# Block-diagonal gate products of a recurrence: one head on 128 rows of the array, or two heads on 64 rows each

## The chip, the cores and the metric

The kernel runs on one core of a Trainium2 chip. The metric is the device time of one execution in microseconds; the median of three runs stands for a kernel. One more execution was recorded by the hardware profiler. Busy time, waits and the order of events below come from that recording. Its engines are TensorE (PE, with its weight loads shown apart as PEld), VectorE (DVE), ScalarE (ACT), GpSimd (POOL) and SyncE (SP), which issues most of the DMAs.

## The reference

One layer of a hybrid backbone is computed for 128 prompt tokens and 512 latent tokens together (640 columns), width 1024. After a norm and the input projection one branch is a bidirectional gated linear recurrence (RG-LRU); beside it run a gated linear attention (GLA) and, behind both, an output projection and an MLP. What is touched here are the recurrence's two gates, a block-diagonal product with 16 blocks (heads) of 64 by 64 per direction:

```
def blockdiag(x, w):
    xb = x.reshape(*x.shape[:-1], LRU_BLOCKS, LRU_BW)      # 16 heads of 64
    return jnp.einsum('...nc,ncd->...nd', xb, w).reshape(x.shape)

r = sigmoid(blockdiag(xc, wa) + ba);  i = sigmoid(blockdiag(xc, wx) + bx)
a = exp(-8 * r * softplus(-L));       u = sqrt(1 - a * a) * (i * xc)
h[t] = a[t] * h[t-1] + u[t]           # forwards and backwards; the two are added
```

All arithmetic of the reference is float32.

## The kernel before

**Matrix products in parts.** A float32 operand is split in two parts of the faster type float32r: a high part (a cast on ACT) and the rest (a subtraction on DVE). A dense product is three matmuls, high by high, high by low, low by high. The dense work of this stretch is the input projection: `dense<-HH,whi`, `dense<-HL,whi`, `dense<-HH,wlo` on 128 rows, 128 columns and 320 tokens each, in PSUM tiles of their own pool (`psd`, two tiles).

**The recurrence.** Features lie on partitions. A group `f` of 128 features holds two heads `b` of 64; there are eight groups and two directions `d`, so 16 pairs (f, d), called directions below. `lru_chain` makes for each group a `prep` stage, two `gates` stages and then decay, inputs, drive and scans. `prep(f)` loads the weights of both heads and directions, gate r and gate i side by side, into `bdr` (the load for the next group is issued by `bd_load`, from POOL after the first group). For each head the 64 features of `xc[f]` are laid on 128 partitions: the high part on the head's own half (`A.copy`), the low part on the other half (`V.tensor_tensor`); this tile is `xs`. The head's weights stand on both halves of `bdr`, split into `bh` and `bl`. So a matmul with `bh` gives the high weights by (high + low) input and one with `bl` the low weights by the same: four products in two matmuls over the full 128 rows, for one head. `gates(f, d)` does this for both heads, each in one tile of the PSUM pool `psa`, which has two tiles named `aux` and serves the GLA stages and transposes too. Each head's result is 64 rows of r over 64 rows of i; a sigmoid on ACT takes it out of PSUM, and three DMAs on SP put the halves together, so that `r` and `i` hold 128 features each.

**The order of the work.** All operations are recorded first, then a planner (`Recorder.order`) goes through them with an estimated cost for each (`Recorder.cost`) and a model of free tiles, and so writes the order of each engine's queue. PE, ACT, DVE and SP then run their queues strictly in that order. All instructions of the profile therefore carry the line of one helper, L343 (L342 for some table loads). The planner lets a matmul of the gates go as soon as an `aux` tile is thought free, between the dense matmuls.

The steps that the change touches are the tile `bdr` and `bd_load` (from line 673), `prep` (line 1102) and `gates` (line 1116) in `lru_chain`, and the planner's cost of a float32r matmul (line 138).

Of the kernel before, what the change touches and what calls it, by code (L numbers as in the profile page):

```python
# [8 lines left out]
F32 = mybir.dt.float32  # L9
F32R = mybir.dt.float32r  # L10
I32 = mybir.dt.int32
AF = mybir.ActivationFunctionType
OP = mybir.AluOpType
# [5 lines left out]
T = 640  # L19
# [90 lines left out]
class Recorder:  # L110
# [21 lines left out]
    @staticmethod  # L132
    def cost(eng, name, args, kw, out):
        n = _dims(out)
        if eng == "PE":
            if name == "transpose":
                return max(0.05, n * 2 / 2400)
            if args[1].dtype == F32R:
                return max(n / 2400 + 0.0025, 0.106)
            if out.ap[0][1] <= 32 and n >= 128:  # L140
                return n / 2400 + 0.0025
            return max(0.213, n * 4 / 2400)
        aps = [a for a in list(args[1:]) + list(kw.values()) if hasattr(a, "ap")]
        scalars = sum(_dims(a) == 1 for a in aps) if n > 1 else 0
        sbuf = all(a.space == bass.MemoryType.SB for a in aps)
        if eng == "ACT":
            if name == "dma_start":
                return 0.1
            return (0.093 if sbuf else 0.051) + n / 1200 + 0.094 * scalars
        if eng == "DVE":  # L150
            if name == "reciprocal":
                return 6.25e-3 * n
            fast = name in ("tensor_copy", "tensor_scalar", "memset") and sbuf and out.space == bass.MemoryType.SB
            return 0.068 + n / (1920 if fast else 960) + 0.061 * scalars
        if eng == "POOL":
            if name == "dma_start":
                return 1.0
            if name in ("memset", "affine_select"):
                return 0.03 + n * 0.0009
            if name == "tensor_copy":  # L160
                return 0.1 + n * 0.0034
            return 0.1 + n * (0.008 if name == "tensor_scalar" and n < 64 else 0.0022) + (0.35 if kw.get("op") == OP.pow else 0.06)
        return 0.63 if kw["in_"].space == bass.MemoryType.SB else 0.5
# [228 lines left out]
def tile_hybrid_layer(  # L392
# [8 lines left out]
    V, A, PE, G, SP = (Port(rec, e) for e in ("DVE", "ACT", "PE", "POOL", "SP"))  # L401

    consts = ctx.enter_context(tc.tile_pool(name="consts", bufs=1))
# [11 lines left out]
    def t_(name, dt=F32):  # L415
        return rec.tile(tp, N_T, [128, TW], dt, name, "t")
# [7 lines left out]
    def aux():  # L424
        return rec.tile(psa, 2, [128, 2, 512], F32, "aux", "a")
# [10 lines left out]
    f32 = lambda ap: ap.bitcast(F32)  # L436
# [83 lines left out]
    ps = aux()  # L520
# [21 lines left out]
    ps = aux()  # L542
# [61 lines left out]
    def split_act(src, hi, lo):  # L604
        A.copy(hi, src)
        V.tensor_tensor(lo, src, f32(hi), op=OP.subtract)
# [63 lines left out]
        by[MH_ENG[3]].tensor_tensor(HL[:, k, :], x[:, 0:T], f32(HH[:, k, :]), op=OP.subtract)  # L670


    bdr = consts.tile([128, 2, 2, 128], F32, name="bdr")

    def bd_load(f):
        for g, w in enumerate((lru_wa, lru_wx)):
            for b in range(2):
                for r in range(2):
                    (G if f else SP).dma_start(out=bdr[64 * r:64 * (r + 1), b, :, 64 * g:64 * (g + 1)],
                                             in_=w[0, :, 2 * f + b].rearrange("d c e -> c d e"))  # L680


    n8sp = consts.tile([128, 16], F32, name="n8sp")
# [74 lines left out]
    units, posted = [], set()  # L758
# [25 lines left out]
    xc, ya = [None] * KT, [None] * KT  # L784
# [161 lines left out]
    def parts(src, name):  # L946
        n = src.shape[-1]
        hi, lo = t_(name + "h", F32R), t_(name + "l", F32R)
        split_act(src, hi[:, 0:n], lo[:, 0:n])
        return hi, lo  # L950
# [147 lines left out]
    def lru_chain(j):  # L1098
        s = {}
        fs = (2 * j, 2 * j + 1)  # L1100

        def prep(f):
            def fn():

                bh, bl, xs = t_("bh", F32R), t_("bl", F32R), (t_("xs", F32R), t_("xs", F32R))
                split_act(bdr.rearrange("p b d e -> p (b d e)"), bh[:, 0:512], bl[:, 0:512])
                for b, x in enumerate(xs):
                    hi, lo = slice(64 * b, 64 * (b + 1)), slice(64 * (1 - b), 64 * (2 - b))
                    A.copy(x[hi, 0:T], xc[f][hi, 0:T])
                    V.tensor_tensor(x[lo, 0:T], xc[f][hi, 0:T], f32(x[hi, 0:T]), op=OP.subtract)  # L1110
                s["in", f] = (bh, bl, xs)
                if f + 1 < KT:
                    bd_load(f + 1)
            return Stage(fn, 2.1, 2.0, lambda: f"zx{f}" in posted)

        def gates(f, d):
            def fn():
                bh, bl, xs = s["in", f]
                out = []
                for b in range(2):  # L1120
                    ps, m = aux(), slice(128 * (2 * b + d), 128 * (2 * b + d + 1))
                    for n, w in enumerate((bh, bl)):
                        for i in range(2):
                            PE.matmul(ps[:, i, 0:320], w[:, m], xs[b][:, 320 * i:320 * (i + 1)], start=n == 0, stop=n == 1)
                    g = t_("r")
                    act(h2(g), pv(ps), AF.Sigmoid, bias=bgate(d, 2 * f + b))
                    out.append(g)

                r, i_, th = out[0], t_("i"), t_("th")
                top, end = slice(0, 64), slice(64, 128)  # L1130
                SP.dma_start(out=i_[top, 0:T], in_=r[end, 0:T])
                SP.dma_start(out=i_[end, 0:T], in_=out[1][end, 0:T])
                SP.dma_start(out=r[end, 0:T], in_=out[1][top, 0:T])
                act(th[:, 0:T], r[:, 0:T], AF.Tanh, scale=p4sp[:, 8 * d + f:8 * d + f + 1])
                V.tensor_tensor(i_[:, 0:T], i_[:, 0:T], xc[f][:, 0:T], op=OP.mult)
                s["r", f, d], s["i", f, d], s["th", f, d] = r, i_, th
            return Stage(fn, 0.75, 2.5)

        def decay():
            for f in fs:  # L1140
                for d in range(2):
                    r = s["r", f, d]
                    act(r[:, 0:T], r[:, 0:T], AF.Exp, scale=n8sp[:, 8 * d + f:8 * d + f + 1])

        def inputs():
            for f in fs:
                for d in range(2):
                    th = s["th", f, d]
                    act(th[:, 0:T], th[:, 0:T], AF.Sqrt)

        def drive(f):
            def fn():
                for d in range(2):
                    r, i_, th = s["r", f, d][:, 0:T], s["i", f, d][:, 0:T], s["th", f, d][:, 0:T]
                    V.scalar_tensor_tensor(th, r, 1.0, th, op0=OP.add, op1=OP.mult)
                    V.tensor_tensor(th, th, i_, op=OP.mult)
            return Stage(fn, 3.0, 0.0)

        def scans(f):
            def fn():  # L1160
                for d in range(2):
                    a, u, h = s["r", f, d], s["th", f, d], s["i", f, d]
                    for sl, init in ((slice(0, 128), 0.0), (slice(128, T), h0(d, f))):
                        av, uv, hv = a[:, sl], u[:, sl], h[:, sl]
                        if d:
                            av, uv, hv = av[:, ::-1], uv[:, ::-1], hv[:, ::-1]
                        V.tensor_tensor_scan(hv, av, uv, init, op0=OP.mult, op1=OP.add)
                    e = 127 * (1 - d)
                    V.tensor_copy(nst[:, 8 * d + f:8 * d + f + 1], h[:, e:e + 1])
                ya[f] = s["i", f, 0]  # L1170
                V.tensor_tensor(ya[f][:, 0:T], ya[f][:, 0:T], s["i", f, 1][:, 0:T], op=OP.add)
                if f == KT - 1:
                    ps = aux()
                    PE.transpose(ps[0:16, 0, 0:128], nst, ident)
                    o = t_("nsto")
                    V.tensor_copy(o[0:16, 0:128], ps[0:16, 0, 0:128])
                    SP.dma_start(out=new_lru[0, 0].rearrange("d (k p) -> (d k) p", p=128), in_=o[0:16, 0:128])
            return Stage(fn, 2.5, 0.0)

        prev = lru_list[-1] if lru_list else None  # L1180
        lru_list.append(Chain("lru", [
            prep(fs[0]), gates(fs[0], 0), gates(fs[0], 1), prep(fs[1]), gates(fs[1], 0), gates(fs[1], 1),
            Stage(decay, 0.0, 2.9), Stage(inputs, 0.0, 2.9), drive(fs[0]), drive(fs[1]), scans(fs[0]), scans(fs[1])],
            after=lambda: prev is None or prev.done))
# [658 lines left out]
```

## Time and profile before

| | |
|---|---|
| median of three runs | 1139.33 us (1138.63 to 1140.05) |
| profiled execution | 1140.71 us, span 1138.8 us |
| PE busy | 1109.5 us, 97% of the span, 7020 matmuls |
| ACT busy | 616.1 us (54%) |
| DVE busy | 848.1 us (74%) |
| gates: matmuls | 128, from 72.8 to 239 us |

The span is the time from the first to the last instruction; the profiled execution's own time is 1.9 us more. Matmuls overlap in the array, so the duration of one (about 310 ns for 320 columns) isn't what it costs; the distance between the starts of two that follow each other is. A wait in the profile is idle time of an engine together with what ended it.

### The profile page before, as it was taken

To read this page: it belongs to the slowest core of one execution; us is meant where nothing else is said; L and a number is where in the kernel's file an instruction comes from. 1 tells how busy PE (TensorE), PEld (TensorE's weight loads), DVE (VectorE), ACT (ScalarE), POOL (GpSimd) and SP (SyncE) were. 2 spreads that over 40 slices of the span, in tenths; PEclk is the share of its full clock that TensorE was granted. 3 is DMA by queue.
4 is the path that set the end of the run, shared out by engine and by line. 5 is a ranking of instruction groups with operands and counts; after the bars stand their busy time and mean duration, and the time that the engine had idled before them with its cause. 6 is when DMAs were issued, how large, how long until landed. Compare 5 with 4: busy or idle time off the path is not lost.

```text
span 1138.8 us, 17811 instructions
## 1 busy us (share of the span) xinstructions
PE 1109.5 (97%) x7020; PEld 1042.9 (92%) x7020; DVE 848.1 (74%) x1363; ACT 616.1 (54%) x998; POOL 78.6 (7%) x152
## 2 busy tenths in 40 slices
PE   6999999999999999999999999999999999999996
PEld 5799898999999999999999988888898899899895
DVE  4686875868474837727996559997779989987767
ACT  5387988895475748611433358744444433333442
POOL 3135103000000000000000011000000000000001
PEclk9999999999999999999999999999999999999998
DMA  9835426251221212227544456422233333222422
GB/s 293 265 74 150 122 66 173 56 163 38 94 75 56 75 57 74 75 74 232 195 157 167 130 184 207 145 75 74 74 123 122 110 118 137 95 75 74 154 88 93
DMA packets 104476, 136.94 MB, mean 120 GB/s; under 512 B 8179, under 2 KB 78021, under 8 KB 104393
## 3 DMA queue, kind: packets, MB, share of 16 engines
q1 hardware_dynamic: 102344, 133.91, 37.8%
q0 software_dynamic: 2048, 1.90, 0.7%
q8 instruction: 55, 0.90, 0.3%
q14 instruction: 29, 0.23, 0.1%
HBM read 121.61 MB, written 6.31 MB: 112 GB/s over the span
## 4 chain that ended last, share of the span: by engine, by line
PE 77%; DVE 9%; ACT 6%; DMA 4%; issue 3%; POOL 0%; SPq 0%; DVEq 0%; POOLq 0%; ACTq 0%
PE dense L343 52%; PE aux L343 25%; DVE i L343 3%; DVE th L343 2%; DMA modw<-in_w_mod_dram 1%; DVE wlo L343 1%; ACT r L343 1%; DMA i<-r 1%; ACT L343 1%; ACT th L343 1%; DMA r<-r 1%; DMA raw<-in_w_in_dram 1%; DMA w2raw<-in_gla_w_dram 1%; ACT whi L343 1%; ACT L342 1%
## 5 line engine op out<-in xcount | busy, mean ns | idle before, releaser
L343 ACT CAST whi<-raw 128x1024 fp32r<-128x1024 f32 (+2 forms) x173 | 167.1, 970 | 289.3 <-PE dense L343 141.5
L343 DVE TENSOR_TENSOR wlo<-raw,whi 128x1024 fp32r<-128x1024 f32 (+1 forms) x168 | 190.1, 1133 | 75.8 <-ACT whi L343 75.0
L343 PE MATMUL dense<-HH,whi 128*128 128x320 f32 x768 | 179.0, 313 | 0.5 <-DVE g L343 0.3
L343 PE MATMUL dense<-HL,whi 128*128 128x320 f32 x768 | 176.5, 310 | 0.0
L343 PE MATMUL dense<-HH,wlo 128*128 128x320 f32 x752 | 172.8, 310 | 0.0
L343 PEld LDWEIGHTS dense<-HH,whi 128*128 128x128 f32 x768 | 129.2, 189 | 2.6 <-issue 0.8
L343 PEld LDWEIGHTS dense<-HL,whi 128*128 128x128 f32 x768 | 129.4, 189 | 0.0
L343 PEld LDWEIGHTS dense<-HH,wlo 128*128 128x128 f32 x752 | 126.4, 189 | 0.0
L343 PE MATMUL dense<-whi,ah 128*128 128x512 f32 (+1 forms) x288 | 113.0, 392 | 0.0
L343 PE MATMUL dense<-wlo,ah 128*128 128x512 f32 (+1 forms) x288 | 113.0, 392 | 0.0
L343 PE MATMUL dense<-whi,al 128*128 128x512 f32 (+1 forms) x288 | 113.0, 392 | 0.0
L343 DVE SCALAR_TENSOR_TENSOR mac<-mw,cst,mac 128x512 f32<-128x512 f32 x112 | 78.1, 746 | 0.0
L343 PE MATMUL aux<-H2H,whi 128*128 128x320 f32 (+1 forms) x240 | 74.8, 311 | 0.0
L343 PE MATMUL aux<-H2L,whi 128*128 128x320 f32 (+1 forms) x240 | 74.7, 311 | 0.0
L343 PE MATMUL aux<-H2H,wlo 128*128 128x320 f32 (+1 forms) x240 | 74.6, 311 | 0.0
L343 PEld LDWEIGHTS dense<-whi,al 128*128 128x128 f32 x288 | 54.1, 188 | 12.5
L343 PEld LDWEIGHTS dense<-whi,ah 128*128 128x128 f32 x288 | 54.1, 188 | 10.3
L343 PEld LDWEIGHTS dense<-wlo,ah 128*128 128x128 f32 x288 | 54.1, 188 | 10.2
L343 ACT CAST whi<-s 128x512 fp32r<-128x512 f32 x42 | 26.0, 619 | 67.1 <-PE aux L343 62.9
L343 PE MATMUL aux<-f,whi 128*128 128x320 f32 x224 | 59.4, 308 | 0.0
L343 DVE TENSOR_TENSOR fa<-fa,dense 128x512 f32<-128x512 f32 x66 | 45.2, 686 | 17.8 <-PE dense L343 17.6
L343 PE MATMUL aux<-f,wlo 128*128 128x320 f32 x168 | 51.9, 309 | 0.0
(335 smaller groups left out, 2500.1 us busy)
## 6 DMA issues: line engine op xcount, KB each, us to landing
raw<-in_mlp_w_dram SPq DMA_DIRECT2D x34, 1024.0 KB, 5.0
raw<-in_w_in_dram SPq DMA_DIRECT2D x24, 1024.0 KB, 5.3
mw<-in_w_mod_dram SPq DMA_DIRECT2D x64, 256.0 KB, 5.4
modw<-in_w_mod_dram SPq DMA_DIRECT2D x32, 256.0 KB, 5.9
raw<-in_w_out_dram SPq DMA_DIRECT2D x8, 1024.0 KB, 4.8
i<-r SPq DMA_DIRECT2D x32, 160.0 KB, 2.4
raw<-in_w_in_dram SPq DMA_DIRECT2D x8, 512.0 KB, 4.6
raw<-in_lru_up_dram SPq DMA_DIRECT2D x4, 1024.0 KB, 4.9
```

The source lines that it names most:

```text
L342: nc.scalar.preload_act_table_set("natural_log_exp_and_others")
L343: getattr(eng[o.eng], o.name)(*o.args, **o.kw)
```

## The change

The two heads of a group are no longer multiplied one after the other over 128 rows. Each head gets 64 rows of the array: `xc[f]` is split as it stands, into `xsh` and `xsl` with both heads on their own halves, and so are the weights, now without the second copy (`bdr`, `bh`, `bl` have 256 columns in place of 512, and a group's weights come in four DMAs in place of eight). A direction then takes three products for each head, 12 matmuls of 64 rows in place of 8 of 128 rows, in which the two heads alternate. Both PSUM tiles are taken at the start, and the sigmoids follow behind all 12. The low-by-low product, which before came along, is left out. The planner gets a cost for a float32r matmul of 64 rows: half that of its columns.

```
             if name == "transpose":
                 return max(0.05, n * 2 / 2400)
+            if args[1].dtype == F32R and args[1].ap[0][1] == 64 and n >= 128:
+                return n / 4800 + 0.0025
...
-    bdr = consts.tile([128, 2, 2, 128], F32, name="bdr")
+    bdr = consts.tile([128, 2, 128], F32, name="bdr")
...
-                for r in range(2):
-                    (G if f else SP).dma_start(out=bdr[64 * r:64 * (r + 1), b, :, 64 * g:64 * (g + 1)],
-                                             in_=w[0, :, 2 * f + b].rearrange("d c e -> c d e"))
+                (G if f else SP).dma_start(out=bdr[64 * b:64 * (b + 1), :, 64 * g:64 * (g + 1)],
+                                           in_=w[0, :, 2 * f + b].rearrange("d c e -> c d e"))
...
-                bh, bl, xs = t_("bh", F32R), t_("bl", F32R), (t_("xs", F32R), t_("xs", F32R))
-                split_act(bdr.rearrange("p b d e -> p (b d e)"), bh[:, 0:512], bl[:, 0:512])
-                for b, x in enumerate(xs):
-                    hi, lo = slice(64 * b, 64 * (b + 1)), slice(64 * (1 - b), 64 * (2 - b))
-                    A.copy(x[hi, 0:T], xc[f][hi, 0:T])
-                    V.tensor_tensor(x[lo, 0:T], xc[f][hi, 0:T], f32(x[hi, 0:T]), op=OP.subtract)
-                s["in", f] = (bh, bl, xs)
+                bh, bl = t_("bh", F32R), t_("bl", F32R)
+                split_act(bdr.rearrange("p d e -> p (d e)"), bh[:, 0:256], bl[:, 0:256])
+                s["in", f] = (bh, bl) + parts(xc[f][:, 0:T], "xs")
...
-                for b in range(2):
-                    ps, m = aux(), slice(128 * (2 * b + d), 128 * (2 * b + d + 1))
-                    for n, w in enumerate((bh, bl)):
-                        for i in range(2):
-                            PE.matmul(ps[:, i, 0:320], w[:, m], xs[b][:, 320 * i:320 * (i + 1)], start=n == 0, stop=n == 1)
+                out, pss, m = [], [aux(), aux()], slice(128 * d, 128 * (d + 1))
+
+                for n, (w, x) in enumerate(((bh, xh), (bh, xl), (bl, xh))):
+                    for i in range(2):
+                        for b, ps in enumerate(pss):
+                            r = slice(64 * b, 64 * (b + 1))
+                            PE.matmul(ps[:, i, 0:320], w[r, m], x[r, 320 * i:320 * (i + 1)], start=n == 0, stop=n == 2)
+                for b, ps in enumerate(pss):
                     g = t_("r")
                     act(h2(g), pv(ps), AF.Sigmoid, bias=bgate(d, 2 * f + b))
```

The planner's order changes with it. Two places on PE show the two forms that a direction takes. The first is group 1, forward, among the dense matmuls of the input projection; before:

```order
L343 MATMUL dense<-HL,whi 128x320 x2
L343 MATMUL dense<-HH,wlo 128x320 x2
L343 MATMUL aux<-xs,bh 128x320 x2
L343 MATMUL aux<-xs,bl 128x320 x2
L343 MATMUL aux<-xs,bh 128x320 x2
L343 MATMUL aux<-xs,bl 128x320 x2
L343 MATMUL dense<-HH,whi 128x320 x2
```

and in the changed kernel, whose helper has line 345:

```order
L345 MATMUL dense<-HL,whi 128x320 x2
L345 MATMUL dense<-HH,wlo 128x320 x2
L345 MATMUL aux<-xsh,bh 128x320 x4
L345 MATMUL aux<-xsl,bh 128x320 x4
L345 MATMUL aux<-xsh,bl 128x320 x4
L345 MATMUL dense<-HH,whi 128x320 x2
```

Eight matmuls in a row have become twelve, and the four of a row go to the heads in turn: head 0, head 1, head 0, head 1. 12 of the 16 directions stand in this way; one of them is in two pieces with dense matmuls between, and in another the first four go head 0 twice, head 1 twice.

The second place is group 2, backward, where the numbers tell the two heads' PSUM tiles apart (305 and 307 before, 310 and 311 now); before:

```order
L343 MATMUL aux_305<-xs_290,bh_288 128x320 x2
L343 MATMUL aux_305<-xs_290,bl_289 128x320 x2
L343 MATMUL dense_299<-HH_127,whi_282 128x320
L343 MATMUL aux_307<-xs_291,bh_288 128x320 x2
L343 MATMUL aux_307<-xs_291,bl_289 128x320 x2
L343 MATMUL dense_299<-HH_127,whi_282 128x320
```

and in the changed kernel:

```order
L345 MATMUL aux_310<-xsh_290,bh_288 128x320 x2
L345 MATMUL aux_310<-xsl_291,bh_288 128x320 x2
L345 MATMUL aux_310<-xsh_290,bl_289 128x320 x2
L345 MATMUL dense_304<-HH_127,wlo_283 128x320
L345 MATMUL dense_321<-whi_286,HH_127 128x256
L345 MATMUL dense_321<-wlo_287,HH_127 128x256
L345 MATMUL aux_311<-xsh_290,bh_288 128x320 x2
L345 MATMUL aux_311<-xsl_291,bh_288 128x320 x2
L345 MATMUL aux_311<-xsh_290,bl_289 128x320 x2
```

Here the planner lets head 0 go as soon as its tile is free and head 1 later, with dense matmuls between: six matmuls on one half of the array, then six on the other. Four directions stand in this way (the tiles 233/234, 310/311, 399/400 and 466/467).

The third place is the queue of SP around group 5, whose halves are put together by the DMAs `i<-r` and `r<-r`; `raw` is a load of weights of 1 MB. Before (direction backward, r_368 and r_370 are the two heads):

```order
L343 DMA r_359<-r_361 64x640
L343 DMA i_371<-r_368 64x640
L343 DMA raw_376<-in_w_in_dram 128x8x256
L343 DMA i_371<-r_370 64x640
L343 DMA r_368<-r_370 64x640
L343 DMA raw_401<-in_w_in_dram 128x8x256
```

and in the changed kernel (r_380 and r_381):

```order
L345 DMA r_362<-r_363 64x640
L345 DMA raw_377<-in_w_in_dram 128x8x256
L345 DMA i_382<-r_380 64x640
L345 DMA i_382<-r_381 64x640
L345 DMA r_380<-r_381 64x640
L345 DMA raw_408<-in_w_in_dram 128x8x256
```

The load that stood between the first and the second DMA of the exchange stands ahead of all three.

## Rows read from the trace of the kernel before

**Rows 1.** The page: busy time of each engine, share of the span, instructions.

```profile
PE 1109.5 (97%) x7020; PEld 1042.9 (92%) x7020; DVE 848.1 (74%) x1363; ACT 616.1 (54%) x998; POOL 78.6 (7%) x152
PE 77%; DVE 9%; ACT 6%; DMA 4%; issue 3%; POOL 0%; SPq 0%; DVEq 0%; POOLq 0%; ACTq 0%
```

**Rows 2.** Stretches with gates: busy by engine (instructions), granted clock, DMA share.

```profile
60.00:120.00 60.00, 60.00 (x411) 59.92 (x410) 47.88 (x70) 49.65 (x76) 25.41 (x57) 1.00 0.47 122
120.00:180.00 60.00, 57.02 (x397) 56.11 (x396) 48.32 (x68) 52.09 (x61) 9.30 (x16) 0.97 0.46 113
180.00:245.00 65.00, 61.34 (x429) 60.47 (x428) 48.34 (x71) 59.01 (x72) 4.68 (x8) 0.97 0.44 116
```

**Rows 3.** Waits of PE, 60 to 245 us: total, times, longest.

```profile
PE aux L343 <- ACT r L343: 6.0, 4, 2.7
PE dense L343 <- DVE g L343: 0.3, 1, 0.3
```

**Rows 4.** Instructions on `xs` and `bh`: count, ns least/median/most, first and last start.

```profile
L343 PE MATMUL aux<-xs,bh x64: 302/309/634, 72.8 to 239.0; 128*128 128x320 f32 x64
L343 PE MATMUL aux<-xs,bl x64: 303/309/468, 73.1 to 239.3; 128*128 128x320 f32 x64
L343 ACT CAST xs<-xc x16: 710/725/733, 67.7 to 221.7; 64x640 fp32r<-64x640 f32 x16
L343 DVE TENSOR_TENSOR xs<-xc,xs x16: 818/820/883, 71.1 to 225.0; 64x640 fp32r<-64x640 f32 x16
L343 ACT CAST bh<-bdr x8: 605/613/624, 46.9 to 216.5; 128x512 fp32r<-128x512 f32 x8
L343 DVE TENSOR_TENSOR bl<-bdr,bh x8: 681/688/693, 47.6 to 223.4; 128x512 fp32r<-128x512 f32 x8
```

**Rows 5.** PE in order of time: one direction (start us, us, instruction).

```profile
113.94 0.46 PE L343 MATMUL aux<-xs,bh 128*128 128x320 f32 x2
114.23 0.45 PE L343 MATMUL aux<-xs,bl 128*128 128x320 f32 x2
...
115.11 0.46 PE L343 MATMUL dense<-HH,whi 128*128 128x320 f32 x2
```

**Rows 6.** PE in order of time: matmuls on a quarter of the array's columns (128*32).

```profile
38.12 0.46 PE L343 MATMUL dense<-HH,wlo 128*128 128x320 f32 x2
38.62 1.93 PE L343 MATMUL aux<-modw,cst 128*32 128x256 f32 x32
40.48 0.56 PE L343 MATMUL dense<-HH,whi 128*128 128x320 f32 x2
40.88 0.31 PE L343 MATMUL dense<-HL,whi 128*128 128x320 f32 x1
...
44.85 0.45 PE L343 MATMUL aux<-HH,whi 128*128 128x320 f32 x2
45.23 1.93 PE L343 MATMUL aux<-modw,cst 128*32 128x256 f32 x32
47.10 0.56 PE L343 MATMUL aux<-HL,whi 128*128 128x320 f32 x2
47.50 0.31 PE L343 MATMUL aux<-HH,wlo 128*128 128x320 f32 x1
```

**Rows 7.** PE in order of time: float32 matmuls, then float32r, all on the full array.

```profile
299.15 0.60 PE L343 MATMUL aux<-sb,ep 128*128 128x256 f32 x2
299.59 0.59 PE L343 MATMUL aux<-sa,ep 128*128 128x256 f32 x2
...
300.32 0.46 PE L343 MATMUL dense<-HL,whi 128*128 128x320 f32 x2
```

**Rows 8.** PE behind two waits, and the clock behind the second (PEclk).

```profile
122.39 0.83 PE L343 MATMUL aux<-xs,bh 128*128 128x320 f32 x2 [1.84 <-ACT r L343]
...
126.09 0.46 PE L343 MATMUL dense<-HH,whi 128*128 128x320 f32 x2
...
183.90 0.90 PE L343 MATMUL aux<-xs,bh 128*128 128x320 f32 x2 [2.71 <-ACT r L343]
...
183.90:187.30 3.40, 3.40 (x13) 0.51 0.27 68
```

**Rows 9.** ACT in order of time: three casts of 256 columns.

```profile
78.55 1.02 ACT L343 CAST whi<-raw 128x256 fp32r<-128x256 f32 x3
```

**Rows 10.** ACT ahead of the wait at 183.90.

```profile
178.61 0.80 ACT L343 ACTIVATE r<-aux,C 128x640 f32<-128x640 f32 x1
182.34 0.83 ACT L343 ACTIVATE th<-r,p4sp 128x640 f32<-128x640 f32 x1 [2.94 <-DMA r<-r]
183.07 0.78 ACT L343 ACTIVATE r<-aux,C 128x640 f32<-128x640 f32 x1
```

**Rows 11.** DMA, 165 to 186 us: queue shares, then issues (KB, us to landing).

```profile
q1 hardware_dynamic: 3757, 4.45, 80.9%
q0 software_dynamic: 256, 0.26, 8.0%
...
bdr<-in_lru_wa_dram POOLq DMA_DIRECT2D x4, 32.0 KB, 8.0
```

More of the change, by code (lines that the diff above doesn't have):

```diff
@@ L1103, in fn @@
             def fn():
-                bh, bl, xs = t_("bh", F32R), t_("bl", F32R), (t_("xs", F32R), t_("xs", F32R))
-                split_act(bdr.rearrange("p b d e -> p (b d e)"), bh[:, 0:512], bl[:, 0:512])
-                for b, x in enumerate(xs):
-                    hi, lo = slice(64 * b, 64 * (b + 1)), slice(64 * (1 - b), 64 * (2 - b))
-                    A.copy(x[hi, 0:T], xc[f][hi, 0:T])
-                    V.tensor_tensor(x[lo, 0:T], xc[f][hi, 0:T], f32(x[hi, 0:T]), op=OP.subtract)
-                s["in", f] = (bh, bl, xs)
+                bh, bl = t_("bh", F32R), t_("bl", F32R)
+                split_act(bdr.rearrange("p d e -> p (d e)"), bh[:, 0:256], bl[:, 0:256])
+                s["in", f] = (bh, bl) + parts(xc[f][:, 0:T], "xs")
                 if f + 1 < KT:
                     bd_load(f + 1)
-            return Stage(fn, 2.1, 2.0, lambda: f"zx{f}" in posted)
+            return Stage(fn, 1.1, 1.0, lambda: f"zx{f}" in posted)
         def gates(f, d):
             def fn():
-                bh, bl, xs = s["in", f]
-                out = []
-                for b in range(2):
-                    ps, m = aux(), slice(128 * (2 * b + d), 128 * (2 * b + d + 1))
-                    for n, w in enumerate((bh, bl)):
-                        for i in range(2):
-                            PE.matmul(ps[:, i, 0:320], w[:, m], xs[b][:, 320 * i:320 * (i + 1)], start=n == 0, stop=n == 1)
+                bh, bl, xh, xl = s["in", f]
+                out, pss, m = [], [aux(), aux()], slice(128 * d, 128 * (d + 1))
[5 more added lines that the diff above has]
+                for b, ps in enumerate(pss):
                     g = t_("r")
```

## The prediction, made before the changed kernel was run

> **What bounds the kernel now.** I read the page first: PE is busy for 97% of the span, and the chain that ended last runs through PE for 77% [rows 1]. So what PE loses or gains per direction is the first question. Then the stretches in which the gates run, 60 to 245 us [rows 2]: PE is idle for 6.6 us of these 185 (the stretches less their PE busy times), ACT is busy for 161 us and in the last stretch for 91%, and the granted clock is 0.97 in two of them where it is 1.00 in the first. The waits of PE there [rows 3] say where the idle time goes: 6.0 us in four waits for `r`, the sigmoid that empties an `aux` tile. Two of them [rows 8] have a second price: behind the wait at 183.90 the granted clock is 0.51, the lower of the two levels (1.2 GHz of 2.4), for 3.4 us, in which 13 matmuls run that take 13 x 0.146 = 1.9 us at the full clock: 1.5 us lost. The one at 122.39 has 14 matmuls in 3.70 us until 126.09, where 2.05 would do: 1.65 lost. So these waits cost 6.0 + 1.5 + 1.65 = 9.2 us in all. The reader is to see two budgets: PE time per direction, and some 9 us that ACT takes from PE because two PSUM tiles come free late.
>
> **PE time of a direction.** Between 113.94 and 115.11 a direction takes 1.17 us for eight matmuls, 0.146 each [rows 5]; the 128 matmuls [rows 4] stand for 16 x 1.17 = 18.7 us. The changed kernel has twelve of 64 rows each. If the two halves of the array work at the same time, a pair takes the 0.146 of one, and a direction in which the heads alternate 6 x 0.146 = 0.88 us: 0.29 less, for 12 directions 3.5 us less. In the other four directions head 0's six stand apart from head 1's, nothing pairs up, and twelve cost 1.75 us: 0.58 more each, 2.3 us more. Left: 1.2 us less.
>
> Does the trace show parts of the array at work together? Not rows, but columns: the 32 `modw` matmuls on a quarter of the columns take 1.87 us, from 45.23 to 47.10 [rows 6], 0.058 each, where a float32 matmul of the same 256 columns on the whole array takes 0.22 (two in 0.44, from 299.15 to 299.59 [rows 7]). Four ran at once, at the full gain. I take the same for two row halves.
>
> **The change of shape.** The same rows show a price. Ahead of the `modw` block the two matmuls before it take 0.38 us (44.85 to 45.23) and not 0.29; the block itself is 1.87 where eight groups of 0.22 are 1.76; the two behind it take 0.40 (47.10 to 47.50). That is 0.09 + 0.11 + 0.11 = 0.31 us for one visit to the split array and back. It isn't the change from float32r to float32 that costs this: from 299.59 to 300.32 two float32 and two float32r matmuls on the whole array take 0.73 us = 0.44 + 0.29, and nothing is lost [rows 7]. The other visit, at 38.62, costs 0.21 + 0.10 + 0.11 = 0.42 in the same sum, where a wait of PE may be in the first term. In the new order I count 21 visits: 12 directions in one visit, one more for the one in two pieces, and four directions in two visits each. At 0.31 us this is 6.5 us. Bounds: nothing, since no row here shows a split by rows, up to 21 x 0.42 = 8.8. I take 6.5, from the only rows that show a split array among dense matmuls.
>
> The Trainium skill, TensorEngine Tiling (Array Packing), Key Properties, says that a change of tiling mode, unlike a change of tile, drains the engine; that speaks against this change, and the `modw` rows agree with it at 0.31 us a visit, though for columns. By that rule the 6.5 us stand; without it the PE sum would be the 1.2 us gain.
>
> PE sum: -3.5 + 2.3 + 6.5 = +5.3 us.
>
> **What leaves ACT, DVE and the queues.** `xs` was cast in two halves of 64 partitions, 16 casts of 0.725; now 8 casts of 128 partitions with the same 640 columns: 5.8 us less on ACT. `bh` falls from 512 to 256 columns: 0.613 against 0.34 (three casts of 256 columns in 1.02 us [rows 9]), eight times 0.27 = 2.2 us. ACT has 8.0 us less. On DVE 8 x 0.82 = 6.6 go from `xs` and about 8 x 0.3 = 2.3 from `bl` [rows 4]: 8.9 us less; for `bl` I take 0.4 us, an estimate between half and all of its 0.688. Of the 64 weight loads into `bdr` 32 go; while the second long wait builds up, such loads hold 8% of the DMA engines that another 81% keep full, and take 8.0 us to land [rows 11]. The sigmoids, tanh, exchanges and table loads stay as many as they were.
>
> None of this is on the path by itself. Its worth is in the 9.2 us of waits: ACT has 8.0 us less to do and PE 5.3 more between 60 and 245 us, so PE comes later to each tile and ACT earlier. Shared out over 16 directions that is 0.8 us each, more than the two shorter of the four waits (6.0 - 2.71 - 1.84 = 1.45 for both). What stays is the kind at 183.90. There a sigmoid stands on ACT behind a tanh, which waited 2.94 us for a DMA of the exchange [rows 10]; queued behind are all of ACT's work and, through the `aux` tile, PE. In the new order a tanh again stands between the two heads' sigmoids (r_394, th_383, r_395), and a load of 1 MB stands ahead of its exchange, so I don't take that one away. And a direction now takes both tiles at once. I take half of the 9.2 us as gone, -4.6. Bounds: all of it (-9.2), or one wait more like that at 183.90 (+2.7 + 1.5 = +4.2).
>
> **Sum.** +5.3 - 4.6 = +0.7 us on the profiled execution's 1140.71: 1141.4. That execution is 1.4 us above the median of the runs; on the median, 1139.33 + 0.7 = 1140.0 us. A difference below 0.2% (2.3 us) can't be told from none here, so this is a forecast of about no change, and the gain in matmuls goes into the changes of shape.
>
> **Rivals.** *No price for the change of shape.* A split by rows leaves all 128 columns as they are, and the weights of a half might be loaded while the whole array still works, as loads are hidden in the dense stream; the `modw` price would then be one of columns. PE is -1.2, the waits give 4.6 (PE isn't later now, so perhaps less): -5.8 to -4, 1134.5 us. For it: each half has its own rows. Against it: the rows of `modw`, the only ones there are.
>
> *Weight loads bound the pairs.* Every matmul has its own load. Behind `modw` one load stands unhidden, and the two matmuls take 0.11 us more [rows 6]. If that is what a load of 128 columns takes and the halves' loads can't overlap, a paired direction takes 12 x 0.11 = 1.32 and not 0.88 us, +5.3 us for twelve: +0.7 + 5.3 = +6.0, 1145.3. For it: in the `modw` block a load has only 32 columns, so it doesn't show four full loads side by side. The Trainium skill, TensorE: Matmul & The Clock Gate, LDWEIGHTS (loading the stationary operand), says that a load's time goes by columns and not by rows, so half the rows save nothing; by it alone two loads for a pair would be as long as here. No row shows two loads of halves.
>
> *The halves don't work together.* Then the twelve paired directions cost 1.75 and not 0.88: +10.5 more, +11.2 in all, 1150.5. Against it: the `modw` quarters, which did.
>
> *More waits for the tiles.* Before, head 0's sigmoid ran while PE was at head 1, and its tile was free half a direction earlier; now both come free after the twelfth matmul, the two sigmoids (0.79 us each) run one after the other, and the next direction can begin only with one of them done and pair up only with both. This decides where ACT is late anyway, from about 120 us on; at +4.2 in place of -4.6 the time is 1139.33 + 5.3 + 4.2 = 1148.8. Against it: directions are mostly 3 us or more apart, and ACT has 8 us less.
>
> **Chances.** The forecast 0.46 (its own range 1136.5 to 1144: waits gone wholly or hardly at all); no price 0.24; weight loads 0.12; no overlap 0.08; more waits 0.10. Of the forecast's 0.46 I put 0.07 below 1137.0, 0.25 within 0.2%, 0.14 above 1141.6. No price is faster but for 0.01; the three slow rivals are slower but for 0.01. Faster: 0.07 + 0.23 = 0.30. Same: 0.25 + 0.02 = 0.27. Slower: 0.14 + 0.29 = 0.43. The range for 8 in 10 goes from the no-price case to nearly the dearest: 1133.5 to 1149.5.
>
> **What would show it.** In the trace of the changed kernel: twelve `aux<-xsh`/`xsl` matmuls that alternate should start in pairs a few ns apart and take about 0.88 us for the block (1.3 with weight loads as the bound, 1.75 without overlap); those of a single head 0.146 apart; the first dense matmul behind a block late by 0.1, and some 0.3 us lost per visit; casts of `xsh` 8 times at 0.72 us; and PE's waits for `r` at half of their 6.0 us or less, with at most one stretch at the lower clock. The prediction is wrong if a visit costs under 0.1 us, if pairs don't pair, or if the waits for `r` grow.

## The result, and the profile after

The changed kernel takes 1144.72 us (median of 6 runs, 1143.71 to 1145.67), the kernel before 1138.98 us beside it (6 runs, 1137.19 to 1142.50): 5.7 us more, ratio 1.0055 [1.0041, 1.0069]. The forecast was about no change, +0.7 us, in a range that reaches to 1149.5. The time lies inside the range, 4.7 us above the point, but just outside the range of the forecast's own case (1136.5 to 1144), and the difference is clear of what the forecast called none (2.3 us). The part of the forecast that spoke of PE's work was right in kind and too small, the part that spoke of waits too hopeful.

The profiled execution took 1143.92 us, its span is 1142.2. The page of the changed kernel, answering to [rows 1]:

```profile
PE 1115.0 (98%) x7084; PEld 1041.9 (91%) x7084; DVE 838.9 (73%) x1355; ACT 609.9 (53%) x990; POOL 63.1 (6%) x124
PE 72%; DVE 4%; ACT 3%; issue 1%; POOL 0%; DVEq 0%; POOLq 0%; ACTq 0%
```

ACT lost 6.2 us and DVE 9.2, as forecast in kind; PE is busy 5.5 us longer. The three stretches with gates, with the columns of [rows 2]:

```profile
60.00:120.00 60.00, 58.61 (x405) 55.66 (x404) 41.80 (x63) 43.88 (x68) 18.41 (x35) 1.00 0.37 97
120.00:180.00 60.00, 59.40 (x438) 57.00 (x437) 51.04 (x72) 52.45 (x65) 4.70 (x8) 1.00 0.45 120
180.00:245.00 65.00, 62.00 (x440) 58.86 (x440) 43.50 (x68) 58.91 (x72) 2.35 (x4) 0.97 0.46 121
```

PE's idle time there is 185 - 180.0 = 5.0 us where it was 6.6. Its waits from 60 to 245 us, answering to [rows 3]:

```profile
PE dense L345 <- DVE vb L345: 2.7, 1, 2.7
PE dense L345 <- ACT zp L345: 1.4, 1, 1.4
PE dense L345 <- DVE g L345: 0.6, 1, 0.6
PE aux L345 <- ACT r L345: 0.3, 1, 0.3
```

The waits for `r` fell from 6.0 us to 0.3. In their place stand waits for tiles of the other PSUM pool, `dense`, which a copy or activation empties late: 4.7 us, where there were 0.3.

What a direction costs PE, the two heads in turn (answers to [rows 5]; start, us, instruction):

```profile
80.31 0.46 PE L345 MATMUL dense<-HH,wlo 128*128 128x320 f32 x2
80.70 0.57 PE L345 MATMUL aux<-xsh,bh 64*128 64x320 f32 x4
81.11 0.46 PE L345 MATMUL aux<-xsl,bh 64*128 64x320 f32 x4
81.40 0.46 PE L345 MATMUL aux<-xsh,bl 64*128 64x320 f32 x4
81.79 0.56 PE L345 MATMUL dense<-HH,whi 128*128 128x320 f32 x2
82.19 0.46 PE L345 MATMUL dense<-HL,whi 128*128 128x320 f32 x2
```

Four matmuls start in the 0.29 us in which two did (81.11 to 81.40): two pairs, the members of each 3 ns apart. The halves of the array do work together. (In the other paired blocks the members start 0 to 17 ns apart, and in the one at 172.57 about 72 ns; that block alone costs 0.06 us more.) The four changes of pitch around the block are the price of the visit: the two dense matmuls ahead take 0.39 us and not 0.29, the first four gates 0.41, the last four 0.39, the first two dense matmuls behind 0.40. That is 0.10 + 0.12 + 0.10 + 0.11 in rounded rows; by the distances of the starts themselves, 0.39 to 0.41 us in the undisturbed blocks. So an undisturbed block with its visit costs 1.27 to 1.29 us, more than the 1.17 before, where the matmuls alone would be 0.88. The loads of weights around the same block show where the price arises:

```profile
80.17 0.33 PEld L345 LDWEIGHTS dense<-HH,wlo 128*128 128x128 f32 x2
80.70 0.30 PEld L345 LDWEIGHTS aux<-xsh,bh 64*128 64x128 f32 x4 [0.20 <-issue]
81.79 0.30 PEld L345 LDWEIGHTS dense<-HH,whi 128*128 128x128 f32 x2 [0.19 <-issue]
```

Among the dense matmuls a load starts one matmul ahead of its own (80.17 for the matmul at 80.31). At both changes of shape it starts together with its own (80.70 and 81.79), after PEld stood idle for 0.20 and 0.19 us, and the first matmul then lasts 0.42 us where the later ones last 0.31. So in this trace the load is not hidden where the shape changes; what holds it back is not shown. A head by itself:

```profile
75.12 0.31 PE L345 MATMUL dense<-HH,wlo 128*128 128x320 f32 x1
75.36 0.56 PE L345 MATMUL aux<-xsh,bh 64*128 64x320 f32 x2
75.76 0.45 PE L345 MATMUL aux<-xsl,bh 64*128 64x320 f32 x2
76.05 0.45 PE L345 MATMUL aux<-xsh,bl 64*128 64x320 f32 x2
76.43 0.42 PE L345 MATMUL dense<-HH,wlo 128*128 128x320 f32 x1
```

Six matmuls 0.146 to 0.15 apart and the same four prices: 1.28 us for one head, 2.55 for the direction.

The casts, answering to [rows 4]:

```profile
L345 ACT CAST xsh<-xc x8: 715/723/731, 67.9 to 215.8; 128x640 fp32r<-128x640 f32 x8
...
L345 ACT CAST bh<-bdr x8: 388/398/407, 45.9 to 215.6; 128x256 fp32r<-128x256 f32 x8
L345 DVE TENSOR_TENSOR bl<-bdr,bh x8: 418/426/475, 47.1 to 224.7; 128x256 fp32r<-128x256 f32 x8
```

**Where the longest new wait comes from.** PE ends a paired block and then waits 2.70 us for a `dense` tile:

```profile
218.36 0.46 PE L345 MATMUL aux<-xsh,bl 64*128 64x320 f32 x4
221.51 0.56 PE L345 MATMUL dense<-HH,whi 128*128 128x320 f32 x2 [2.70 <-DVE vb L345]
```

DVE empties that tile with the copy to `vb`. Its queue in the changed kernel, then at the same place in the kernel before:

```profile
218.85 0.14 DVE L345 COPY nst<-i 128x1 f32<-128x1 f32 x1
218.90 1.23 DVE L345 TENSOR_TENSOR wlo<-raw,whi 128x1024 fp32r<-128x1024 f32 x1
220.03 0.83 DVE L345 TENSOR_TENSOR i<-i 128x640 f32<-128x640 f32 x1
220.76 0.70 DVE L345 COPY vb<-dense 128x512 f32<-128x512 f32 x1
```

```profile
215.27 0.13 DVE L343 COPY nst<-i 128x1 f32<-128x1 f32 x1
215.32 0.68 DVE L343 COPY vb<-dense 128x512 f32<-128x512 f32 x1
215.91 0.82 DVE L343 TENSOR_TENSOR i<-i 128x640 f32<-128x640 f32 x1
216.65 1.22 DVE L343 TENSOR_TENSOR wlo<-raw,whi 128x1024 fp32r<-128x1024 f32 x1
```

Before, the copy stood directly behind the recurrence's scans and the small copy to `nst`; now two operations of 1.13 and 0.73 us by their starts stand ahead of it, and the scans end 3.6 us later. By these lengths 1.86 of the 2.70 us are the planner's placing of those two.

### The profile page after: what moved, and what is told of

Same layout as the page of the kernel before. It is cut to its first block, busy times and chain, and to the rows that moved or that the text cites. A ratio compares the mean times of both kernels' runs of the same rounds, so it can differ in the third digit from the quotient of the medians.

```text
span 1142.2 us, 17855 instructions
## 1 busy us (share of the span) xinstructions
PE 1115.0 (98%) x7084; PEld 1041.9 (91%) x7084; DVE 838.9 (73%) x1355; ACT 609.9 (53%) x990; POOL 63.1 (6%) x124
## 4 chain that ended last, share of the span: by engine, by line
PE 72%; DVE 4%; ACT 3%; issue 1%; POOL 0%; DVEq 0%; POOLq 0%; ACTq 0%
PE dense L345 49%; PE aux L345 23%; ACT junk L345 1%; ACT ab L345 1%; DVE ab L345 1%; DVE wlo L345 1%; ACT whi L345 0%; DVE la L345 0%; DVE fb L345 0%; DVE fa L345 0%; ACT hx L345 0%; DVE i L345 0%; ACT L344 0%; ACT L345 0%; DVE ot L345 0%
```

## The experiments

The account used for all of them: until the first matmul on `yash` (the next product's operand) everything differs, behind it the kernels run alike, 671.5 to 672.6 us to the end in all but e12 (677.2). Ahead of it, from 60 us on, the matmuls that are no gates take 357.7 to 359.0 us by their columns in every trace. So three terms tell kernels apart: PE's work on the gates (0.88 us for a paired direction, 1.75 for one whose heads go alone, 0.39 for a visit, as the blocks that no wait disturbs show them; for e2 the length of its blocks), PE's idle time, and stretches of 3.4 us at the lower clock, each worth some 1.6 us. What is left over is 17 to 19 us everywhere, most of it float32 matmuls that take longer than their columns say (0.215 us for 256 columns, where float32r ones take 0.117). "Idle" below is that of this stretch.

| kernel | median us | ratio to before | gates' PE us | idle us | low stretches | first `yash` |
|---|---|---|---|---|---|---|
| before | 1138.98 | 1 | 18.7 | 7.7 | 2 | 466.3 |
| changed | 1144.72 | 1.0055 [1.0041, 1.0069] | 26.2 | 6.5 | 1 | 469.9 |
| changed, again | 1144.56 | 1.0056 [1.0043, 1.0068] | 26.2 | 6.7 | 0 | 468.0 |
| e1 | 1137.19 | 0.9988 [0.9978, 0.9998] | 21.5 | 4.8 | 0 | 463.0 |
| e2 | 1138.15 | 0.9993 [0.9984, 1.0003] | 27 | 2.0 | 0 | 465.2 |
| e3 | 1143.57 | 1.0057 [1.0038, 1.0076] | 21.1 | 8.0 | 1 | 467.8 |
| e13 | 1146.49 | 1.0079 [1.0066, 1.0093] | 21.5 | 12.1 | 3 | 474.8 |
| e6 | 1136.81 | 0.9985 [0.9975, 0.9994] | 18.7 | 5.4 | 2 | 463.0 |
| e12 | 1166.05 | 1.0252 [1.0238, 1.0267] | 18.7 | 21.1 | 5 | 486.4 |

Theory: the pairs work, but visits to the split array and heads left alone cost PE more than pairing gives, and this shows in full in the time (A where a letter stands for it). Rivals: both tiles taken at once make the waits; the relief of ACT and DVE is what moves the time; the order that the planner writes decides, whatever the matmuls are.

**e1: every direction paired.** The first matmul of a direction now asks the planner for both tiles:

```
                             PE.matmul(ps[:, i, 0:320], w[r, m], x[r, 320 * i:320 * (i + 1)], start=n == 0, stop=n == 2)
+                            if n == i == 0:
+                                rec.ops[-1].tiles.append(pss[1 - b].tensor.name)
```

> The changed kernel, but the planner may start a direction only when both PSUM tiles are free, so that all 16 directions stand in pairs (19 visits to the split array in place of 21, no six matmuls on one half alone). Theory A, that the time is in PE's own work (0.39 us a visit in the trace of the changed kernel, and 0.88 us for every unpaired direction): 4 x 0.88 + 2 x 0.39 = 4.3 us less than the changed kernel, 1140 to 1141 us, +0.1% to +0.2% on the kernel before. Theory B, that taking both tiles at once is what costs (PE waits for sigmoids): the waits grow and the time stays at 1144 us or above.

1137.19 us (11 runs): 7.5 us less than the changed kernel, 3 more than the theory gave. All 16 directions pair, in 19 visits; the gates take 21.5 us of PE, 4.7 less. Idle time fell as well:

```profile
PE aux L345 <- DVE nst L345: 1.5, 1, 1.5
PE dense L345 <- ACT q L345: 0.8, 1, 0.8
PE aux L345 <- ACT r L345: 0.7, 2, 0.5
```

The direction is the theory's, and taking both tiles at once does not make waits for `r`. But PE's work explains at most 4.7 of the 7.5 us: added up from the actual starts, e1's blocks take 22.9 us, as some visits are lengthened by a wait, and that is 3.2 less than the changed kernel's 26.2. The rest lies in waits and the clock, and e3 and e13 below show that the same matmuls in other orders don't keep the gain.

**e2: as e1, with one head's six matmuls written ahead of the other's.**

```
-                for n, (w, x) in enumerate(((bh, xh), (bh, xl), (bl, xh))):
-                    for i in range(2):
-                        for b, ps in enumerate(pss):
+                for b, ps in enumerate(pss):
+                    for n, (w, x) in enumerate(((bh, xh), (bh, xl), (bl, xh))):
+                        for i in range(2):
```

> As e1_both_tiles, but with the loop over heads outside: six matmuls of head 0, then six of head 1, in the same visits. If the two halves really work together, this undoes it: 16 x 0.88 = 14 us more than e1_both_tiles, 1152 to 1155 us, a little less where PE's longer work covers waits. If the halves gave nothing, the same as e1_both_tiles.

A miss: 1138.15 us, about 1 more than e1. It did not do what it was meant to, since the planner mixed the heads again:

```profile
83.35 0.56 PE L345 MATMUL aux<-xsh,bh 64*128 64x320 f32 x2
83.76 0.31 PE L345 MATMUL aux<-xsl,bh 64*128 64x320 f32 x1
83.77 0.41 PE L345 MATMUL aux<-xsh,bh 64*128 64x320 f32 x1
83.91 0.31 PE L345 MATMUL aux<-xsl,bh 64*128 64x320 f32 x1
84.02 0.31 PE L345 MATMUL aux<-xsh,bh 64*128 64x320 f32 x1
```

Head 0's third matmul starts with head 1's first, so four of the six pair up, and a block costs 1.69 us, not the 2.14 of no overlap. Even so PE has 4.6 to 5.5 us more work than in e1 (by the starts, by the table), and 1.0 us shows between the medians, 2.0 between the profiled executions: idle time fell from 4.8 to 2.0. PE's work takes the place of waits.

**e8 and e8c: a visit by itself, and its control.** In the kernel before, one short matmul per direction into columns that nothing reads; on 64 rows, and in the control on 128:

```
+                    if b == 0:
+                        PE.matmul(ps[:, 0, 384:512], bh[0:64, m], xs[b][0:64, 0:128], start=True, stop=True)
```

> The kernel before with one matmul more in each direction: 64 rows by 128 columns, written into columns of the PSUM tile that nothing reads; it only brings the array into the split shape and back. Theory A: 16 x (0.39 + about 0.06 for the matmul) = 7 us more on PE, 5 to 7.5 us in the time (PE's waits cover some). Theory B (a change of shape is not what costs): the same as e8c_no_visit, +1 us.

> The control for e8_visit_alone: the same extra matmul of 128 columns, with all 128 rows. Both theories: 16 x 0.06 to 0.11 us = 1 to 2 us more than the kernel before, or within noise of it.

1141.14 us, ratio 1.0014 [1.0005, 1.0023], and 1138.97 us, 1.0008 [0.9997, 1.0018]. The same direction on 64 rows, then on 128:

```profile
116.50 0.45 PE L343 MATMUL dense<-HH,wlo 128*128 128x320 f32 x2
116.88 0.82 PE L343 MATMUL aux<-xs,bh 64*128 64x128 f32 x3
117.54 0.45 PE L343 MATMUL aux<-xs,bl 128*128 128x320 f32 x2
```

```profile
116.59 0.45 PE L343 MATMUL dense<-HH,wlo 128*128 128x320 f32 x2
116.88 0.57 PE L343 MATMUL aux<-xs,bh 128*128 128x128 f32 x3
117.29 0.46 PE L343 MATMUL aux<-xs,bl 128*128 128x320 f32 x2
```

Entry 0.38 and not 0.29, the three gates 0.66 and not 0.41: 0.34 us for a visit of one matmul, by the whole block 1.625 against 1.286. So it is the number of rows that costs, nothing else of the change, and the rival without a price falls. The Trainium skill, TensorEngine Tiling (Array Packing), Key Properties, says that a change of tiling mode drains the engine; a price of 0.34 us for a change of rows agrees with that. In time the visits show less than was expected (5 to 7.5 us): outside idle time and the lower clock the stretch is 4.9 us longer than in the control, but its idle time is 3.8 where the control has 6.6 us, and 2.2 us are left between the medians.

**after_again: the changed kernel once more.**

> The changed kernel a second time, beside the others and with a second trace. If its waits (2.70 us for the DVE copy vb, 1.39 us for the ACT copy zp, 0.6 us for DVE g) come from the order of its queues, they stand at the same instructions again and the time is again 0.4 to 0.7% above the kernel before. If they are chance (DMA landings), they stand elsewhere and the difference shrinks towards that of e2_one_half_at_a_time, about nothing.

1144.56 us, and the waits stand at the same instructions with the same lengths (0.58 for `g`, 2.68 for `vb`, 1.39 for `zp`): the order of the queues makes them, not chance. One thing differs: the clock behind the wait for `vb`, which ends at 221.51 us in the first trace and at 220.92 in the second. The same 3.4 us of both spans, first trace first (the first number after POOL's count is the granted clock):

```profile
221.51:224.91 3.40, 3.40 (x15) 3.40 (x16) 3.40 (x5) 3.37 (x5) 0.00 (x0) 0.60 0.43 96
```

```profile
221.51:224.91 3.40, 3.40 (x25) 3.40 (x24) 3.40 (x6) 3.37 (x4) 0.00 (x0) 1.00 0.51 109
```

15 matmuls against 25; the second trace has no stretch at the lower clock from 60 us to its first `yash` at all. The same wait is followed by the lower clock in one execution and not in the other, and their times are 1143.92 and 1141.99.

**e3 and e13: e1's matmuls in other orders.** e3 is e1 with a planner that adds 0.195 us where the rows change; e13 is e1 without the planner's new cost, so that it takes a matmul of 64 rows for as long as a whole one:

```
+            if e == "PE":
+                rows = o.args[1].ap[0][1] == 64 and o.name == "matmul"
+                us += 0.195 * (rows != halves)
+                halves = rows
...
-            if args[1].dtype == F32R and args[1].ap[0][1] == 64 and n >= 128:
-                return n / 4800 + 0.0025
```

> As e1_both_tiles, and the planner adds 0.195 us for each change between the split and the whole array. 18 visits, all paired: PE's work 21.1 us where e1_both_tiles has 21.5 and the kernel before 18.7. If waits follow from a plan that is too quick, they fall below e1's 2.4 us between 60 and 250 us, and the time is 1136 to 1137.5 us. If they follow from the luck of the order, anything within 3 us of e1_both_tiles.

> As e1_both_tiles, without the planner's new cost: again 16 paired directions in 19 visits, PE's work 21.5 us, in another order. If e1's 1137.2 us comes from the pairs, 1136.5 to 1138.5 us here too; if it was the luck of its order, anything up to the 1143.6 us of e3_planner_knows.

Both pair in all directions, in 18 and 19 visits, with 21.1 and 21.5 us of PE's work, as e1; yet they take 1143.57 and 1146.49 us. Waits make the difference. Those of e13 from 60 to 285 us:

```profile
PE aux L343 <- DVE nst L343: 5.5, 1, 5.5
PE dense L343 <- ACT q L343: 2.1, 1, 2.1
PE dense L343 <- ACT vc L343: 1.7, 1, 1.7
```

Both are misses: e3 was expected within 3 us of e1 at most, e13 at 1143.6 or below. Costs nearer to the chip's did not give a better order.

**e12: the kernel before in another order.** Nothing but the planner's cost of a whole float32r matmul is changed:

```
-                return max(n / 2400 + 0.0025, 0.106)
+                return max(n * 0.00045 + 0.002, 0.106)
```

> The kernel before, with the planner's cost of a float32r matmul set to what the trace shows (0.45 ns a column and 2 ns, in place of 0.417 and 2.5): the same instructions, another order. If the order alone is worth some us, it is 1 to 5 us away from the kernel before, up or down; if the order is worth little, within 1 us.

1166.05 us, 27 more than the table's median with the same instructions (28.7 by the ratio, which is against before on the same chip). From 60 to 285 us:

```profile
PE aux L343 <- ACT r L343: 11.5, 4, 4.0
PE dense L343 <- ACT zp L343: 5.1, 3, 2.9
```

Expected were 1 to 5 us, so this is a miss in size. The order alone is worth more than anything in this change; e1 to e13 is 9 us and before to e12 27 us at equal work on PE.

**e6: the kernel before with both tiles at once.** Matmuls of 128 rows as before, e1's two lines, and both sigmoids behind all eight matmuls.

```
-                out = []
-                for b in range(2):
-                    ps, m = aux(), slice(128 * (2 * b + d), 128 * (2 * b + d + 1))
+                out, pss = [], [aux(), aux()]
+                for b, ps in enumerate(pss):
+                    m = slice(128 * (2 * b + d), 128 * (2 * b + d + 1))
...
+                for b, ps in enumerate(pss):
                     g = t_("r")
```

> The kernel before, with a direction that takes both PSUM tiles at its start and has its two sigmoids behind all eight matmuls, as the changed kernel does; PE's work is that of the kernel before (18.7 us). If taking both tiles at once is what costs in the change, PE's waits for r grow beyond 6.0 us and it is 2 to 4 us slower. If not, within 1.5 us of the kernel before.

1136.81 us, 0.9985 [0.9975, 0.9994] of before: faster by little, and the least time of all kernels here. Of the 6.0 us of waits for `r` 0.8 are left (waits of 0.7 us for `nst` and 0.4 for `vc` are not shown):

```profile
PE dense L343 <- ACT zp L343: 3.1, 1, 3.1
PE aux L343 <- ACT r L343: 0.8, 2, 0.5
```

The rival of more waits for the tiles falls: taken together, they make fewer. With both tiles taken at once in either form, the two forms of the matmuls stand 0.4 us apart (e1 1137.19, e6 1136.81), which can't be told from none. Their clocks differ, though: the mean granted clock is 0.993 over e1's 11 runs and 0.9905 over e6's, which is worth 1.2 to 2.8 us in e1's favour (an estimate; how it is made stands under "The sum" below). By this estimate the kernel with 128-row matmuls would be ahead at an equal clock, as its 18.7 us of PE's work let expect.

**e7, e10, e11: what was not shown or only adds to this.** e7 is e3 with the casts and subtractions of `prep` done twice, so that ACT and DVE get their work back; e10 is the kernel before with the casts of `xs` on POOL; e11 is the changed kernel without the planner's new cost.

```
+                for _ in range(2):
+                    A.copy(xh[:, 0:T], xc[f][:, 0:T])
...
-                    A.copy(x[hi, 0:T], xc[f][hi, 0:T])
+                    G.tensor_copy(x[hi, 0:T], xc[f][hi, 0:T])
```

> As e3_planner_knows, but in each group the casts and subtractions of weights and inputs are done twice, which gives ACT back 8 x 1.1 = 9 us and DVE 8 x 1.25 = 10 us, about what the change had taken from them. If that relief is what shrinks PE's waits, they come back: 2 to 5 us more than e3_planner_knows. If not, within 1 us of it.

> The kernel before with the 16 casts of xs on POOL in place of ACT (11.6 us less on ACT; PE's work as before, no split array). If ACT's load is what PE waits for, the 9 us of waits shrink: 3 to 5 us less, 1134 to 1136 us. If the order or DMA landings cause the waits, or the slower POOL casts come late themselves: the same or slower.

> The changed kernel without the planner's new cost for 64-row matmuls, one part of the change undone. The order has 14 paired directions and 2 unpaired in 20 visits, PE's work 26.2 - 2 x 0.88 - 0.39 = 24.0 us. If PE's work alone decides: 2.2 us less than the changed kernel, 1142 us. If the order decides through its waits: anything from 1137 to 1146 us, and the sum of PE's work, idle time and stretches at the lower clock from the trace gives it.

e7: 1144.56 us, 1.0 above e3, inside what the intervals allow (1.0060 [1.0048, 1.0072] against e3's). e10: 1139.79 us, 1.0015 [1.0003, 1.0026]; the waits for `r` went from 6.0 to 4.8 us, the time did not follow. Neither shows a worth of the relief; since either also gets its own order, neither shows that there is none. e11: 1150.17 us, 1.0115 [1.0100, 1.0130], with 14 directions paired, 2 us less of PE's work than the changed kernel, and 8.3 us of waits for `r`: dearer with less to do, and above the 1137 to 1146 us that were expected. One more part of the change bears on the order: the ACT and DVE times that `prep` announces, when the stages are laid out, fall from 2.0 and 2.1 us to 1.0 and 1.1. All kernels built from the changed one keep that, e11 too, so what it does alone was not run.

## Why the prediction was right and wrong, point by point

- **Pairs.** Right: a pair takes 0.147 us, the block of twelve 0.88. The rivals of weight loads as the bound (1.32) and of halves that don't work together (1.75) fall by the block at 80.70. The time itself, 1144.72 us, lies next to the 1145.3 of the rival with weight loads; only the trace tells the two apart. The Trainium skill, TensorE: Matmul & The Clock Gate, LDWEIGHTS (loading the stationary operand), has a load's time go by columns; the recorded loads of 64 rows agree, 0.184 us where 128 rows take 0.188, but the two loads of a pair lie side by side, so by it alone the block came out too dear.
- **Heads alone.** Right: six in 0.88 us, four directions at 1.75.
- **The change of shape** is the term that was mis-sized: 0.31 us a visit from the `modw` rows, 0.40 measured, inside the bounds. 21 visits are 8.3 and not 6.5 us. The `modw` block didn't show one of the four prices: behind the first matmuls on the split array a further 0.10 us goes ahead of the second ones, as behind the return. With `modw` the load that starts with its matmul has 32 columns and takes 0.11 us, here 128 and 0.18; that this is the cause is an argument, not shown. PE's sum came out as +7.5 us (18.7 to 26.2) and not +5.3.
- **Relief.** ACT's casts of `xsh` took 0.723 us each, `bh` 0.398 where 0.34 was put, `bl` 0.426 where 0.4 was: by the lengths of these instructions 7.5 us less on ACT, not 8.0, and 8.7 on DVE, not 8.9. The page's busy time, which counts overlapping instructions once, fell by 6.2 and 9.2.
- **The waits** are the step that failed most in kind: "I take half of the 9.2 us as gone, -4.6". By name it looked better than that, since the waits for `r` went almost wholly. But only 1.65 us of idle time went from 60 to 245 us. The prediction took idle time as something that ACT owes PE for `aux` tiles, and had no term for the other PSUM pool, whose tiles came free late in the new order. It went by the queues of PE, SP and ACT, and not by where DVE's copies to `vb` stand.
- **The clock.** One lower stretch in place of two, 1.7 us, in the profiled execution, and none in the second. As the same wait gave both, such a stretch is scatter between executions, and the 3.15 us of it in the 9.2 had no place in a forecast of the median.
- **The sum.** In the two profiled executions, from 60 us to the first `yash`: PE +7.5, idle -1.2, clock -1.7, remainder -1.0, together +3.6 (406.2 to 409.8). The medians stand 5.7 apart, the profiled execution of before being 1.7 above its median and that of the changed kernel 0.8 below. Without the clock's term the sum is +5.3, near the median's. The granted clock of each run, which is on record, says which way the clock went over many runs: in mean 0.9910 over the six runs of the changed kernel's second set and 0.9924 over 16 runs of the kernel before beside them, where the two profiled executions had 0.992 and 0.990. So the clock went against the change, not for it. These 0.0014 would be 1.6 us if all of it were paid in time; by all runs on record, compared within each kernel, 0.001 of the clock goes with 0.5 us, which gives 0.7 (estimates). With +5.3 that makes 6 to 7 us, near the 5.7 but not equal to it; the sum closes only roughly. That the time lies inside the stated range is in part luck: both terms erred towards too little time, and the range's upper end came from rivals whose mechanisms (loads as the bound, no overlap, more waits for the tiles) the runs refute.

What stays open is how much of the 5.7 us another order of the same twelve matmuls would keep. e1 shows that 7.5 less is possible, e11 that 5.5 more is. The 7.5 us on PE are read from the blocks, but e2 and e8 add some 5 us each to PE, over e1 and over the control, of which 1.0 and 2.2 show. So the time after the change is PE's surplus and one order out of many, and the runs don't split the two further.

## What to carry to other kernels

Two halves of the array give the full factor of two, but each visit to them among matmuls of the whole array cost 0.40 us here: with 0.29 us saved per visit it can't pay on PE, unless several directions share one visit. Where two products are to pair up, make the program take both their tiles at once, or some will go alone. And where a planner writes the order, changing one cost can move waits by more than a few us of work: read every queue that empties a tile, the unconcerned pools' too, and judge an edit over several orders (e1, e3, e13) before its time is called its own.

## What the runs showed that was not expected

- The price of a visit comes in four parts of about 0.1 us, two on the way in (93 and 104 ns over the usual 146 between starts) and two on the way out (90 and 105).
- At a change of shape the weight load starts with its matmul and not one matmul ahead; in the visits that no wait disturbs PEld stands idle for 0.13 to 0.20 us before it.
- Pairing needs no matched starts: in e2 one head's third matmul ran with the other's first.
- A wait of 2.7 us of PE was followed by 3.4 us at the lower clock (1.2 of 2.4 GHz) in one execution and by none in another of the same kernel.
- 27 us, 2.4% of the time, lay in the order of queues alone (e12), at equal instructions.
